# Earlier issue of three x tiles, and a chunk's transposes between the halves of the chunk ahead

## The chip, the cores and the metric

The kernel runs on all 8 cores of one Trainium2 chip, every core with its own data and no communication. The metric is the device time of the slowest core, in microseconds (us). The median before was 841.71 us.

A program on eight cores has a second, slower state: in some executions the cores of one die (cores 0 to 3 or 4 to 7), or of both, get a lower clock for their matrix engine and the time is some per cent longer (about 842 us in fast executions of the kernel before, 868 to 1002 in slow ones; the mean granted clock of a core was 0.98 to 1.00 in fast executions and down to 0.81 in slow ones). Where a profile fell in the slow state, only the cores of the undisturbed die are read.

Names: PE is the TensorE, DVE the VectorE, ACT the ScalarE, POOL the GpSimd engine, SP the engine whose queue issues the tables and most x tiles. SBUF is the memory that the tiles lie in, PSUM the one that matmuls and transposes write. The granted clock is the share of the PE's full clock that the profile records (1.00 is full, 0.50 half).

## The reference, cut to what matters

One layer of a decoder with two gated branches, in float32, with 2048 prompt rows and 64 sample rows per core, so 17 chunks of 128 rows (the last has 64).

```python
h = rms_norm(x, norm_g)
z = h @ w_in                      # nine slices of 1024 columns each
u_a, v_a, gate_a, c_b, b_b, h_b, gate_b, m_a, m_b = split(z)
v_a = layer_norm(gelu(v_a), ln_v_g, ln_v_b)
s   = W_s(group) @ v_a + b_s      # within 128-row chunks
y_a = gelu(u_a) * s * silu(gate_a)
...                               # branch B, merge, output projection, per-layer embedding, final norm
```

The change touches only the first stage of the kernel: normalise x, transpose it (the matmuls of this kernel read h with channels on the partitions), project v, apply GELU and its layer norm. Everything after it starts from the transposed h (`HT`) and the normalised v (`VA`).

## The kernel before

Each engine has one queue of instructions, written out in the order of the Python calls; an instruction waits on semaphores for the buffers that it reads and writes. So the order of calls decides the order on every engine, and that is what the change edits. The helpers of a chunk `c` in the first stage (shortened):

```python
NXI = 6                                   # x tiles in SBUF: tile c lies in slot c % 6
def x_load(c, eng="sp"): ...              # DMA of x rows into XIN[c % 6]
def A0(c): ...  # ACT: square of the tile with row sums; POOL: add eps, power -0.5
def A2(c): ...  # DVE: HTOK = XIN * 1/rms * gain        (1.28 us)
def A3(c): ...  # PE: 8 transposes of HTOK into PSUM
def A4(c): ...  # DVE: copy of the transposes into HT   (0.69 us)
def Bmm(c): ... # PE: 16 matmuls of 512 columns, v of the chunk
def Bact_g(c): ... # ACT: GELU out of PSUM
def Bact_s(c): ... # ACT: square of the GELU with row sums
def C1(c): ...  # DVE: three small operations on the statistics
def C2(c): ...  # POOL: power -0.5
def C3(c): ...  # DVE: one small operation, then VA = normalised v (0.81 us)
```

The opening issues four slices of the v weights and x tiles 2 to 5 on the POOL queue, splits chunk 0 into halves (`A2(0, 0, 1)`, `A2(0, 1, 2)` and so on), and then the sync queue issues four tables before tile 6:

```python
        S._waits("sp", [B_xin[5]], ())    # wait for tile 5
        S.dma("sp", [DMA(cpk[:], cpk_d[:, :])], ...)      # 20 KB
        S.dma("sp", [DMA(bsr[:], ...)], ...)              # 4 KB
        S.dma("sp", [DMA(WST, wsT_d[:, :])], ...)         # 512 KB
        S.dma("sp", [DMA(BC2, ln_b_d.partition_broadcast(128))], ...)   # 512 KB
        ...                                # chunks 0 to 2, slice by slice
        for i in range(4, NCH + 5):
            if 5 <= i - 1 < NCH:
                A2(i - 1)
            if 4 <= i - 2 < NCH:
                A3(i - 2)
                A4(i - 2)
            if 3 <= i - 3 < NCH:
                Bmm(i - 3)
            if okc(i - 5):
                C1(i - 5); C2(i - 5)
            if okc(i - 4):
                Bact_g(i - 4)
            if 5 <= i + 1 < NCH:
                A0(i + 1)
            if okc(i - 4):
                Bact_s(i - 4)
            if okc(i - 5):
                C3(i - 5)
            if NXI <= i + 2 < NCH:
                x_load(i + 2)
            if i == 7: ...    # POOL: select that makes wT from WST
            if i == 8: ...    # DVE: cast of a table to bf16
            if i == 10:
                make_Bd()     # PE: bias table, 16 small matmuls, half of them with one row
            if i == 11: ...   # DVE: copy of the bias table out of PSUM
```

Of the kernel before, what the change touches and what calls it, by code (L numbers as in the profile page):

```python
# [9 lines left out]
ALU = mybir.AluOpType  # L10
# [5 lines left out]
NCH = 17  # L16
# [7 lines left out]
def crow(c):  # L24
    return 128 if c < 16 else 64

def group_chunks(g):
    t0, n = GROUPS[g]
    out = []
    for c in range(NCH):  # L30
        a, b = max(t0, c * 128), min(t0 + n, c * 128 + crow(c))
        if a < b:
            out.append((c, a - c * 128, b - c * 128, a - t0))
    return out
# [119 lines left out]
def STT(out, in0, scalar, in1, op0, op1):  # L154
    return lambda e: e.scalar_tensor_tensor(out=out, in0=in0, scalar=scalar, in1=in1, op0=op0, op1=op1)  # L155
# [6 lines left out]
def CP(out, in_):  # L162
    return lambda e: e.tensor_copy(out=out, in_=in_)
# [7 lines left out]
def build_program(stop_after=99, dbg=()):  # L171
# [31 lines left out]
    with ExitStack() as es:  # L203
# [24 lines left out]
        ps = [es.enter_context(nc.psum_tensor("ps%d" % i, [128, 1024], F32)) for i in range(4)]  # L228
# [7 lines left out]
        S = Sched(nc, es)  # L236
        B_bank = [Buf("bank%d" % i) for i in range(8)]
# [4 lines left out]
        NXI = 6  # L242
        XIN = [MGf[:, i * 1024:(i + 1) * 1024] for i in range(NXI)]
        BC0 = MGf[:, 6144:7168]
        HTOK = [MG[:, 14336:15360], MG[:, 15360:16384], YA[:, 0:1024]]
# [7 lines left out]
        B_xin = [Buf("xin%d" % i) for i in range(NXI)]  # L253
        B_gv = [Buf("gv%d" % i) for i in range(4)]
        B_htok = [Buf("htok0"), Buf("htok1"), Buf("htok2")]
        B_junk = Buf("junk")
        B_bc0h = [Buf("bc0_0"), Buf("bc0_1")]
        B_bc1, B_bc2 = Buf("bc1"), Buf("bc2")
        B_stat = [Buf("stat%d" % c) for c in range(NCH)]
        B_hT = [Buf("hT%d" % c) for c in range(NCH)]  # L260
# [5 lines left out]
        B_ring = [Buf("ring%d" % i) for i in range(NRING)]  # L266
        B_wpp = Buf("wpp")

        def st(c, i, r=128):
            return stat[0:r, c * 16 + i:c * 16 + i + 1]  # L270
# [8 lines left out]
        B_id, B_identb, B_ones, B_blk = Buf("ident"), Buf("identb"), Buf("ones"), Buf("blk")  # L279
# [4 lines left out]
        def x_load(c, eng="sp"):  # L284
            r, t0, sl = crow(c), c * 128, c % NXI
            S.dma(eng, [DMA(XIN[sl][0:r, :], x_d[t0:t0 + r, :])], B_xin[sl] if eng == "sp" else Buf("xsw%d" % c),
                  writes=[B_xin[sl]])
# [6 lines left out]
        def warm(n):  # L294
            S.group("pe", [MM(ps[2][:, 512:1024], JUNK[:, 0:128], JUNK[:, 0:512], True, True) for _ in range(n)], reads=[B_junk])
# [28 lines left out]
        for i, v in ((C_NH, -0.5), (C_DEPS, D * EPS), (C_EPS, EPS)):  # L324
# [4 lines left out]
             writes=[B_id])  # L329
# [7 lines left out]
        for q in range(2):  # L337
            S.op("pe", MM(ps[3][:, q * 512:(q + 1) * 512], ones[0:1, :], GROW[:, q * 512:(q + 1) * 512], True, True),
                 reads=[B_ones, B_gr], writes=[B_bank[6 + q]])
# [10 lines left out]
        HT3 = HT[:, :].rearrange("p (k t) -> p k t", t=NT)  # L350
# [7 lines left out]
            S.op("pool", TT(st(c, 1), st(c, 0), cc(C_EPS), ALU.add), reads=[B_cst], writes=[B_stat[c]])  # L358
            S.op("pool", TT(st(c, 2), st(c, 1), cc(C_NH), ALU.pow), reads=[B_cst], writes=[B_stat[c]])

        def A2(c, q0=0, q1=2):
            r, sl, hs, a, b = crow(c), c % NXI, c % 3, q0 * 512, q1 * 512
            S.op("dve", STT(HTOK[hs][0:r, a:b], XIN[sl][0:r, a:b], st(c, 2, r), BC0[0:r, a:b], ALU.mult, ALU.mult),
                 reads=[B_xin[sl], B_stat[c]] + B_bc0h[q0:q1], writes=[B_htok[hs]])

        def A3(c, q0=0, q1=2):
            r, sl, hs = crow(c), c % 2, c % 3
            pt = bank_bf(sl)
            S.group("pe", [TR(pt[:, k * 128:k * 128 + r], HTOK[hs][0:r, k * 128:(k + 1) * 128], ident[0:r, 0:r])
                           for k in range(4 * q0, 4 * q1)], reads=[B_htok[hs], B_identb], writes=[B_bank[sl]])  # L370

        def A4(c, q0=0, q1=2, own=None):
            r, t0, sl = crow(c), c * 128, c % 2
            pt = bank_bf(sl)
            S.op("dve", CP(HT3[:, 4 * q0:4 * q1, t0:t0 + r],
                           pt.rearrange("p (k t) -> p k t", t=128)[:, 4 * q0:4 * q1, 0:r]),
                 reads=[B_bank[sl]], writes=[own or B_hT[c]])

        B_hT0b = Buf("hT0b")

        def v_pair(c):
            return 1 + c if c < 3 else 1 + (c + 1) % 2
# [1 line left out]
        def Bmm(c, slots=(0, 1, 2, 3)):  # L384
            r, t0, pi = crow(c), c * 128, v_pair(c)
            fns = [MM(ps[pi][0:r, q * 512:(q + 1) * 512], HT[:, k * NT + t0:k * NT + t0 + r],
                      WR[:, k * D + q * 512:k * D + (q + 1) * 512], k == 0, k == 7)
                   for s_ in slots for k in (2 * s_, 2 * s_ + 1) for q in range(2)]
            S.group("pe", fns, reads=[B_hT[c]] + ([B_hT0b] if c == 0 and slots[0] else []) + [B_ring[s_] for s_ in slots],
                    writes=[B_bank[2 * pi], B_bank[2 * pi + 1]] if slots[-1] == 3 else [])  # L390

        def Bact_g(c):
# [57 lines left out]
        x_load(4, "pool")  # L450
        x_load(5, "pool")
        A0(2)
        S._waits("sp", [B_xin[5]], ())
        S.dma("sp", [DMA(cpk[:], cpk_d[:, :])], B_cpk, writes=[B_cpk])
        S.dma("sp", [DMA(bsr[:], b_s_d.rearrange("(o h) t -> o (h t)", o=1))], B_bsr, writes=[B_bsr])
        S.dma("sp", [DMA(WST, wsT_d[:, :])], B_ws, writes=[B_ws])
        S.dma("sp", [DMA(BC2, ln_b_d.partition_broadcast(128))], B_bc2, writes=[B_bc2])

        def bc0(q):
            S.op("dve", CP(BC0[:, q * 512:(q + 1) * 512], ps[3][:, q * 512:(q + 1) * 512]), reads=[B_bank[6 + q]],  # L460
                 writes=[B_bc0h[q]])

        bc0(0)
        A2(0, 0, 1)
        bc0(1)
        A3(0, 0, 1)
        A4(0, 0, 1)
        A2(0, 1, 2)
        Bmm(0, (0,))
        A3(0, 1, 2)  # L470
        A4(0, 1, 2, B_hT0b)
        B_hT[0].inherit(B_hT0b)
        warm(2)
        A2(1)
        A3(1)
        A4(1)
        warm(1)
        Bmm(1, (0,))
        for c in range(2):
            Bmm(c, (1,))  # L480
        A2(2)
        A3(2)
        A4(2)
        for s_ in range(2):
            Bmm(2, (s_,))
        A0(3)
# [10 lines left out]
        for i in range(4, NCH + 5):  # L497
            if 5 <= i - 1 < NCH:
                A2(i - 1)
            if 4 <= i - 2 < NCH:  # L500
                A3(i - 2)
                A4(i - 2)
            if 3 <= i - 3 < NCH:
                Bmm(i - 3)
            if okc(i - 5):
                C1(i - 5)
                C2(i - 5)
# [5 lines that stand above are left out]
                Bact_s(i - 4)  # L513
            if okc(i - 5):
                C3(i - 5)
            if NXI <= i + 2 < NCH:
                x_load(i + 2)
            if i == 7:
                S.op("pool", lambda e: e.affine_select(out=wT3, in_=WST.rearrange("s (h t) -> s h t", t=128),
                                                       pattern=[[0, 8], [1, 128]], compare_op=ALU.is_ge, fill=0.0,  # L520
                                                       base=0, channel_multiplier=-1),
                     reads=[B_ws], writes=[B_wT])
                issue_loads(6)
            if i == 9:
                issue_loads(NRING)
            if i == 8:
                S.op("dve", CP(BC2b, BC2), reads=[B_bc2], writes=[B_bc2b])
            if i == 11:
                S.op("dve", CP(Bd[:, :], ps[3][:, :]), reads=[B_bank[6], B_bank[7]], writes=[B_Bd])
            if i == 10:  # L530
                make_Bd()
                S.dma("sp", [DMA(BC1, ln_g_d.partition_broadcast(128))], B_bc1, writes=[B_bc1])
                S.dma("pool", [DMA(WPP[:, :].rearrange("p (k c) -> p k c", c=D),
                                   w_pp_d.rearrange("(k p) c -> p k c", p=128))], B_wpp, writes=[B_wpp])
            if i == 12:
                emit_blk_dmas()
                S.dma("sp", [DMA(ci_s[:, :], ci0_d[:, :])], B_cis[0], writes=B_cis)

# [9 lines left out]
            return bank(b)[:, 0:GROUPS[g][1]], B_bank[b]  # L548

        def hT_bufs(g):  # L550
            return ([B_hT0b] if g == 0 else []) + [B_hT[c] for (c, _, _, _) in group_chunks(g)]

        def proj(blk_i, c0, g, SRC, src_bufs):
            t0, n = GROUPS[g]
# [19 lines left out]
        if stop_after >= 2:  # L574
# [3 lines left out]
            for h in range(8):  # L578
# [4 lines left out]
                for g in range(5):  # L583
                    t0, n = GROUPS[g]
                    o, ob = proj_hT(bu, hc, g)
                    S.op("act", ACT(T1[:, t0:t0 + n], o, AF.Gelu_apprx_tanh), reads=[ob], writes=[B_t1[g]])
                for g in range(5):
                    t0, n = GROUPS[g]
                    sl = g % 2
# [3 lines left out]
                         reads=[B_t1[g]], writes=[B_t2[sl]])  # L593
                    po, pob = alloc_out(g)
                    fns = []
# [3 lines left out]
                    for (c, la, lb, off) in chs:  # L599
# [4 lines left out]
                        else:  # L604
# [9 lines left out]
                         reads=[pob, B_Bd, B_lngT], writes=[B_tmp[sl]])  # L614
                    if n > npp:
# [3 lines left out]
                             reads=[pob, B_Bd, B_lngT], writes=[B_tmp[sl]])  # L619
                    S.op("dve", TT(YA[:, h * NT + t0:h * NT + t0 + n], tmp[:, 0:n], T2[sl][:, 0:n], ALU.mult),  # L620
                         reads=[B_tmp[sl], B_t2[sl]], writes=[B_ya[h]])
# [6 lines left out]
        if stop_after >= 3:  # L628
# [12 lines left out]
            for j in range(8):  # L641
# [5 lines left out]
                for g in range(5):  # L647
                    t0, n = GROUPS[g]
                    sl = g % 2
# [11 lines left out]
                    else:  # L661
# [5 lines left out]
                         writes=[B_acc[sl]])  # L667
                    S.op("dve", STT(acc[:, 0:npr], ci[:, 1:1 + npr], w1, acc[:, 0:npr], ALU.mult, ALU.add),
                         reads=[B_ci[sl], B_convw], writes=[B_acc[sl]])
                    S.op("dve", STT(acc[:, 0:npr], ci[:, 0:npr], w0, acc[:, 0:npr], ALU.mult, ALU.add),  # L670
                         reads=[B_ci[sl], B_convw], writes=[B_acc[sl]])
                    if g == 4:
                        S.op("pool", CP(cs3[:, j, 0:2], ci[:, npr:npr + 2]), reads=[B_ci[sl]], writes=[B_csall])
                    if has_s:
# [8 lines left out]
                             writes=[B_accs])  # L683
                        S.op("dve", STT(acc3, cj[:, :, 0:4], w0, acc3, ALU.mult, ALU.add), reads=[B_cis[j], B_convw],
                             writes=[B_accs])
# [347 lines left out]
```

## Time and profile before

| | before |
|---|---|
| time, median of the first 3 runs | 841.71 us (841.52 to 842.14) |
| PE busy | 809.4 of 841.0 us (96%) |
| first stage ends | 100.6 us, mean of 8 cores (98.0 to 101.4) |
| longest PE idle time from 38 to 47 us | 3.9 us, mean of 8 cores |

"First stage ends" is, throughout, the start of the first matmul on `ps<-HT,WR`, the next stage's form. The PE never waits long after it (at most 2.04 us at a time before, on core 5, and 1.52 after, on core 7), so a microsecond won in the first stage should be a microsecond of the whole: the mean span less the mean stage end is 837.8 - 100.6 = 737.2 us before, and 834.8 - 98.0 = 736.8 us after.

The timeline of the PE on core 5, the slowest core of this profile, around the first gap. Columns: start in us, duration in us, engine, line (of a helper), operation, output<-inputs, shape, count, and in brackets the idle time before it and what ended it. `L146` are transposes (A3), `ps<-WR,HT` is a chunk's v projection.

```profile
34.85 0.61 PE L146 MATMUL ps<-ident,YA 128*128 128x128 bf16 x8 [0.52 <-DVE YA L155]
35.45 3.61 PE L143 MATMUL ps<-WR,HT 128*128 128x512 bf16 x16
44.45 1.01 PE L146 MATMUL ps<-ident,MG 128*128 128x128 bf16 x8 [5.39 <-DVE MG L155]
45.26 5.50 PE L143 MATMUL ps<-WR,HT 128*128 128x512 bf16 x16
50.60 0.61 PE L146 MATMUL ps<-ident,MG 128*128 128x128 bf16 x8
51.05 3.62 PE L143 MATMUL ps<-WR,HT 128*128 128x512 bf16 x16
...
64.47 6.13 PE L143 MATMUL ps<-WR,HT 128*128 128x512 bf16 x16
70.44 0.61 PE L146 MATMUL ps<-ident,MG 128*128 128x128 bf16 x8
```

The PE stands still for 5.39 us before chunk 6's transposes, and the sixteen matmuls after that take 5.50 us instead of 3.62. The matmuls at 64.47 follow the bias table and are slow too (6.13 us).

The row of the windows view for the same core (window, its length, busy time of PE, weight loads, DVE, ACT, POOL, then granted clock, DMA share, GB/s) shows the clock:

```profile
35.00:45.00 10.00, 4.61 (x30) 2.36 (x29) 3.58 (x10) 6.90 (x13) 2.90 (x5) 0.86 0.96 295
45.00:58.00 13.00, 12.91 (x66) 5.99 (x64) 9.74 (x20) 10.90 (x22) 7.47 (x14) 0.84 1.00 213
```

Why chunk 6 is late is in two more timelines of the same core, first that of the sync queue:

```profile
27.16 0.33 SPq L169 DMA_DIRECT2D cpks<-cpk  x1
27.53 0.42 SPq L169 DMA_DIRECT2D bsr<-b_s  x1
28.00 0.36 SPq L169 DMA_DIRECT2D YA<-wsT  x1
28.40 0.42 SPq L169 DMA_DIRECT2D YA<-ln_b  x1
29.04 15.57 SPq L169 DMA_DIRECT2D MG<-x  x7
```

Then that of ACT, with the square of tile 6:

```profile
38.10 1.06 ACT L149 ACTIVATE MG<-MG 128x1024 bf16<-128x1024 f32 x1 [6.83 <-DMA MG<-x]
```

Tile 5 lands at 27.1, four tables go first, tile 6 is issued at 29.04, and ACT waits 6.83 us for it. The square of tile 6 then starts the chain of statistics, multiply, transposes.

A second thing shows in the same profile, late in the stage: DVE's copies of the transposes (A4).

```profile
75.48 0.68 DVE L163 COPY HT<-ps 128x1024 bf16<-128x1024 bf16 x1
...
77.60 0.16 DVE L155 SCALAR_TENSOR_TENSOR stat<-stat 128x1 f32<-128x1 f32 x1 [0.80 <-POOL stat L152]
...
79.79 0.68 DVE L163 COPY HT<-ps 128x1024 bf16<-128x1024 bf16 x1
```

They follow each other at 4.31 us, with no wait for another engine except 0.80 us in each round for POOL's power (C2). The PE needs 3.9 us for a chunk. Before, nothing was lost by that: between a chunk's transposes and its matmuls stood the sixteen matmuls of the chunk ahead (3.5 us from start to start), so DVE could fall that far behind. Its copy starts 0.72 us after the transposes at 70.44 and 3.0 us after those at 89.94, and soon after that the stage ends.

### The profile page before, as it was taken

Reading aid. Unit: us, or ns where it says so; the run is one execution under the profiler, and the core shown is the slowest. Engines: PE = TensorE matmul, PEld = TensorE weight load, DVE = VectorE, ACT = ScalarE, POOL = GpSimd, SP = SyncE. Lnnn points to the kernel's source line nnn. Section 1 sums busy time; section 2 is a strip of 40 time slices with the busy share of each in tenths; the row PEclk is TensorE's granted clock in tenths of the full one; section 3 lists DMA queues with packets and bytes.
Section 4 is the critical chain, followed back from the end, with each engine's and each line's share of the span. In section 5 each row is a group of like instructions: output and inputs, shape, how many; then the busy total and the mean of one; then the engine's idle time right before and its main releaser. Section 6 shows DMA issues by size and latency. Waiting matters only on the chain.

```text
span 841.0 us, 14209 instructions; the slowest of 8 cores (834.3 to 841.0 us)
## 1 busy us (share of the span) xinstructions
PE 809.4 (96%) x4563; PEld 431.9 (51%) x4563; DVE 445.4 (53%) x728; ACT 301.1 (36%) x517; POOL 117.5 (14%) x257
## 2 busy tenths in 40 slices
PE   5789999999999999999999999999999999999994
PEld 2345455555554555455555545554555454444441
DVE  4376675646665555555555323332333246777774
ACT  2476645554432333232332111111111124545552
POOL 4153210000000100101001001000010012323331
PEclk8988999999999999999999999999999999999998
DMA  9895073302300410600603406005032762344311
GB/s 185 219 219 113 1 140 49 51 13 40 51 1 1 76 26 1 101 1 5 97 1 55 79 1 101 1 12 90 1 57 45 97 191 90 135 148 139 122 76 62
DMA packets 21338, 60.78 MB, mean 72 GB/s; under 512 B 2770, under 2 KB 7058, under 8 KB 21268
## 3 DMA queue, kind: packets, MB, share of 16 engines
q0 software_dynamic: 10352, 29.89, 22.8%
q1 hardware_dynamic: 10914, 29.99, 11.4%
q8 instruction: 40, 0.66, 0.3%
q14 instruction: 30, 0.25, 0.1%
q10 hardware_dynamic: 2, 0.00, 0.0%
HBM read 78.08 MB, written 9.58 MB: 104 GB/s over the span
## 4 chain that ended last, share of the span: by engine, by line
PE 92%; DMA 3%; DVE 1%; ACT 1%; issue 1%; POOL 1%; POOLq 0%; DVEq 0%; SPq 0%; ACTq 0%
PE ps L143 90%; DMA MG<-x 2%; PE ps L146 2%; DMA YA<-pe_g 1%; DVE YA L155 1%; ACT SCR L149 1%; ACT YA L149 0%; POOL stat L152 0%; ACT MG L149 0%; POOL WR L169 0%; DVE MG L155 0%; DVE WR L155 0%; DVE YA L152 0%; DVE VA L155 0%; DVE YA L159 0%
## 5 line engine op out<-in xcount | busy, mean ns | idle before, releaser
L143 PE MATMUL ps<-HT,WR 128*128 128x512 bf16 (+2 forms) x2560 | 469.7, 342 | 0.0
L143 PEld LDWEIGHTS ps<-HT,WR 128*128 128x128 bf16 x2560 | 248.4, 98 | 200.7 <-issue 0.4
L149 ACT ACTIVATE SCR<-ps 128x512 f32<-128x512 f32 (+2 forms) x240 | 123.9, 520 | 324.0 <-PE ps L143 268.4
L155 DVE SCALAR_TENSOR_TENSOR SCR<-SCR,ps 128x512 f32<-128x512 f32 (+2 forms) x80 | 47.5, 594 | 151.2 <-PE ps L143 151.2
L152 POOL TENSOR_TENSOR stat<-stat,cst 128x1 f32<-128x1 f32 x119 | 68.3, 576 | 178.4 <-ACT SCR L149 105.2
L152 DVE TENSOR_TENSOR SCR<-SCR,ps 128x512 f32<-128x512 f32 (+2 forms) x88 | 48.1, 547 | 46.5 <-PE ps L143 38.1
L155 DVE SCALAR_TENSOR_TENSOR SCR<-SCR,cpks 128x512 f32<-128x512 f32 (+1 forms) x80 | 51.5, 644 | 38.0 <-ACT SCR L149 27.8
L143 PE MATMUL ps<-WR,HT 128*128 128x512 bf16 (+1 forms) x272 | 66.8, 402 | 4.2 <-DMA WR<-w_v 2.4
L143 PE MATMUL ps<-HT 128*128 128x512 bf16 (+1 forms) x272 | 61.6, 379 | 2.3 <-ACT HT L149 2.3
L143 PE MATMUL ps<-YA,WR 128*128 128x512 bf16 (+2 forms) x320 | 63.6, 342 | 0.0
L143 PE MATMUL ps<-VA,WR 128*128 128x512 bf16 (+2 forms) x320 | 63.6, 342 | 0.0
L143 PE MATMUL ps<-WR,MG 128*128 128x512 bf16 (+1 forms) x272 | 62.5, 384 | 0.0
L169 POOL DMA_DIRECT2D WR<-wt x44 | 24.0, 546 | 274.3 <-PE ps L143 272.5
L149 ACT ACTIVATE SCR<-SCR,cpks 128x512 f32<-128x512 f32 (+1 forms) x40 | 25.5, 637 | 60.5 <-DVE SCR L152 60.5
L143 PEld LDWEIGHTS ps<-WR,HT 128*128 128x128 bf16 (+1 forms) x272 | 27.2, 103 | 36.9 <-issue 11.8
L152 DVE TENSOR_TENSOR SCR<-SCR 128x512 f32<-128x512 f32 (+2 forms) x40 | 23.7, 592 | 41.5 <-ACT SCR L149 41.5
L143 PEld LDWEIGHTS ps<-VA,WR 128*128 128x128 bf16 x320 | 31.3, 98 | 25.8
L143 PEld LDWEIGHTS ps<-YA,WR 128*128 128x128 bf16 x320 | 31.3, 98 | 25.8
L143 PEld LDWEIGHTS ps<-WR,MG 128*128 128x128 bf16 (+1 forms) x272 | 27.0, 100 | 32.6 <-issue 2.0
L143 PEld LDWEIGHTS ps<-HT 128*128 128x128 bf16 (+1 forms) x272 | 25.9, 98 | 31.0 <-issue 3.3
L155 DVE SCALAR_TENSOR_TENSOR YA<-YA,ps 128x1024 f32<-128x1024 f32 (+1 forms) x17 | 20.7, 1220 | 21.2 <-ACT YA L149 21.2
L152 DVE TENSOR_TENSOR VA<-SCR 128x512 bf16<-128x512 f32 (+2 forms) x48 | 25.2, 526 | 7.7 <-DVE SCR L152 5.0
(85 smaller groups left out, 549.4 us busy)
## 6 DMA issues: line engine op xcount, KB each, us to landing
WR<-wt POOLq DMA_DIRECT2D x44, 512.0 KB, 9.0
y<-YA SPq DMA_DIRECT2D x16, 512.0 KB, 2.9
MG<-x SPq DMA_DIRECT2D x12, 512.0 KB, 9.7
WR<-x SPq DMA_DIRECT2D x8, 512.0 KB, 4.4
VA<-x SPq DMA_DIRECT2D x8, 512.0 KB, 4.3
WR<-w_v POOLq DMA_DIRECT2D x4, 512.0 KB, 12.2
MG<-x POOLq DMA_DIRECT2D x4, 512.0 KB, 14.5
SCR<-p SPq DMA_DIRECT2D x16, 128.0 KB, 4.2
```

Source lines behind the costliest of these rows:

```text
L143: return lambda e: e.matmul(out, lhsT=lhsT, rhs=rhs, start=start, stop=stop)
L146: return lambda e: e.transpose(out, in_, idn)
L149: return lambda e: e.activation(out=out, in_=in_, func=func, **kw)
L152: return lambda e: e.tensor_tensor(out=out, in0=in0, in1=in1, op=op)
L155: return lambda e: e.scalar_tensor_tensor(out=out, in0=in0, scalar=scalar, in1=in1, op0=op0, op1=op1)
L169: return lambda e: e.dma_start(out=out, in_=in_)
```

## The change

Its intent: let the DMA engines fetch tiles 6 to 8 in the pause that the tables' turn left (41 GB/s from 27 to 30 us on core 5, against 295 from 35 to 45), and hide the wait for a chunk's transposes behind the second half of the chunk ahead. The opening works in whole tiles instead of halves, and the table work moves two rounds later. The core of the diff, shortened:

```diff
-        S._waits("sp", [B_xin[5]], ())
+        S._waits("sp", [B_xin[4]], ())
+        for c in range(6, 9):
+            x_load(c)
         S.dma("sp", [DMA(cpk[:], cpk_d[:, :])], B_cpk, writes=[B_cpk])
 ...
-        bc0(0)
-        A2(0, 0, 1)
-        bc0(1)
-        A3(0, 0, 1)
-        A4(0, 0, 1)
-        A2(0, 1, 2)
-        Bmm(0, (0,))
-        ...
+        warm(9)
+        A2(0)
+        A2(1)
+        A3(0)
+        A4(0)
+        A3(1)
+        A4(1)
+        for s_ in range(2):
+            for c in range(2):
+                Bmm(c, (s_,))
 ...
             if 5 <= i - 1 < NCH:
                 A2(i - 1)
+            if 3 <= i - 3 < NCH:
+                Bmm(i - 3, (0, 1))
             if 4 <= i - 2 < NCH:
                 A3(i - 2)
                 A4(i - 2)
             if 3 <= i - 3 < NCH:
-                Bmm(i - 3)
+                Bmm(i - 3, (2, 3))
 ...
-            if NXI <= i + 2 < NCH:
-                x_load(i + 2)
+            if NXI + 3 <= i + 5 < NCH:
+                x_load(i + 5)
 ...          # select i == 7 -> 9, cast 8 -> 10, make_Bd 10 -> 12, its copy 11 -> 13, and so on
```

`Bmm` also got a wait for its PSUM banks at the start of the first half.

More of the change, by code (lines that the diff above doesn't have):

```diff
@@ L359, in A0, with A2, A3 @@
             S.op("pool", TT(st(c, 2), st(c, 1), cc(C_NH), ALU.pow), reads=[B_cst], writes=[B_stat[c]])
-        def A2(c, q0=0, q1=2):
-            r, sl, hs, a, b = crow(c), c % NXI, c % 3, q0 * 512, q1 * 512
-            S.op("dve", STT(HTOK[hs][0:r, a:b], XIN[sl][0:r, a:b], st(c, 2, r), BC0[0:r, a:b], ALU.mult, ALU.mult),
-                 reads=[B_xin[sl], B_stat[c]] + B_bc0h[q0:q1], writes=[B_htok[hs]])
-        def A3(c, q0=0, q1=2):
+        def A2(c):
+            r, sl, hs = crow(c), c % NXI, c % 3
+            S.op("dve", STT(HTOK[hs][0:r, :], XIN[sl][0:r, :], st(c, 2, r), BC0[0:r, :], ALU.mult, ALU.mult),
+                 reads=[B_xin[sl], B_stat[c]] + B_bc0h, writes=[B_htok[hs]])
+        def A3(c):
             r, sl, hs = crow(c), c % 2, c % 3
@@ L369, in A3, with A4 @@
             S.group("pe", [TR(pt[:, k * 128:k * 128 + r], HTOK[hs][0:r, k * 128:(k + 1) * 128], ident[0:r, 0:r])
-                           for k in range(4 * q0, 4 * q1)], reads=[B_htok[hs], B_identb], writes=[B_bank[sl]])
-        def A4(c, q0=0, q1=2, own=None):
+                           for k in range(8)], reads=[B_htok[hs], B_identb], writes=[B_bank[sl]])
+        def A4(c):
             r, t0, sl = crow(c), c * 128, c % 2
             pt = bank_bf(sl)
-            S.op("dve", CP(HT3[:, 4 * q0:4 * q1, t0:t0 + r],
-                           pt.rearrange("p (k t) -> p k t", t=128)[:, 4 * q0:4 * q1, 0:r]),
-                 reads=[B_bank[sl]], writes=[own or B_hT[c]])
-        B_hT0b = Buf("hT0b")
+            S.op("dve", CP(HT3[:, :, t0:t0 + r], pt.rearrange("p (k t) -> p k t", t=128)[:, :, 0:r]),
+                 reads=[B_bank[sl]], writes=[B_hT[c]])
         def v_pair(c):
@@ L388, in Bmm @@
                    for s_ in slots for k in (2 * s_, 2 * s_ + 1) for q in range(2)]
-            S.group("pe", fns, reads=[B_hT[c]] + ([B_hT0b] if c == 0 and slots[0] else []) + [B_ring[s_] for s_ in slots],
+            if slots[0] == 0:
+                S._waits("pe", (), [B_bank[2 * pi], B_bank[2 * pi + 1]])
+            S.group("pe", fns, reads=[B_hT[c]] + [B_ring[s_] for s_ in slots],
                     writes=[B_bank[2 * pi], B_bank[2 * pi + 1]] if slots[-1] == 3 else [])
@@ L452, in build_program @@
         A0(2)
-        S._waits("sp", [B_xin[5]], ())
+        for q in range(2):
+            S.op("dve", CP(BC0[:, q * 512:(q + 1) * 512], ps[3][:, q * 512:(q + 1) * 512]), reads=[B_bank[6 + q]],
+                 writes=[B_bc0h[q]])
+        warm(9)
[8 more added lines that the diff above has]
+                Bmm(c, (s_,))
+        A2(2)
+        A3(2)
+        A4(2)
+        S._waits("sp", [B_xin[4]], ())
+        for c in range(6, 9):
+            x_load(c)
         S.dma("sp", [DMA(cpk[:], cpk_d[:, :])], B_cpk, writes=[B_cpk])
@@ L457, in build_program @@
         S.dma("sp", [DMA(BC2, ln_b_d.partition_broadcast(128))], B_bc2, writes=[B_bc2])
-        def bc0(q):
-            S.op("dve", CP(BC0[:, q * 512:(q + 1) * 512], ps[3][:, q * 512:(q + 1) * 512]), reads=[B_bank[6 + q]],
-                 writes=[B_bc0h[q]])
-        bc0(0)
-        A2(0, 0, 1)
-        bc0(1)
-        A3(0, 0, 1)
-        A4(0, 0, 1)
-        A2(0, 1, 2)
-        Bmm(0, (0,))
-        A3(0, 1, 2)
-        A4(0, 1, 2, B_hT0b)
-        B_hT[0].inherit(B_hT0b)
-        warm(2)
-        A2(1)
-        A3(1)
-        A4(1)
-        warm(1)
-        Bmm(1, (0,))
-        for c in range(2):
-            Bmm(c, (1,))
-        A2(2)
-        A3(2)
-        A4(2)
         for s_ in range(2):
@@ L515, in build_program @@
                 C3(i - 5)
-            if NXI <= i + 2 < NCH:
-                x_load(i + 2)
-            if i == 7:
+            if NXI + 3 <= i + 5 < NCH:
+                x_load(i + 5)
+            if i == 9:
                 S.op("pool", lambda e: e.affine_select(out=wT3, in_=WST.rearrange("s (h t) -> s h t", t=128),
@@ L523, in build_program @@
                 issue_loads(6)
-            if i == 9:
+            if i == 11:
                 issue_loads(NRING)
-            if i == 8:
+            if i == 10:
                 S.op("dve", CP(BC2b, BC2), reads=[B_bc2], writes=[B_bc2b])
-            if i == 11:
+            if i == 13:
                 S.op("dve", CP(Bd[:, :], ps[3][:, :]), reads=[B_bank[6], B_bank[7]], writes=[B_Bd])
-            if i == 10:
+            if i == 12:
                 make_Bd()
@@ L534, in build_program @@
                                    w_pp_d.rearrange("(k p) c -> p k c", p=128))], B_wpp, writes=[B_wpp])
-            if i == 12:
+            if i == 14:
                 emit_blk_dmas()
@@ L550, in hT_bufs @@
         def hT_bufs(g):
-            return ([B_hT0b] if g == 0 else []) + [B_hT[c] for (c, _, _, _) in group_chunks(g)]
+            return [B_hT[c] for (c, _, _, _) in group_chunks(g)]
         def proj(blk_i, c0, g, SRC, src_bufs):
```

## The prediction

> **What bounds it now.** The busy table gives the TensorE 809.4 of 841.0 us (96%); the chain of waits puts 92% of the span on it. What can be won is in the first stage (normalise, transpose, project v), which by the timeline ends at 101.4 us on the slowest core (98.0 to 101.4 by core); the other 737 to 740 us are not touched. A chunk costs the TensorE 3.9 us there, so what follows the start of chunk 4 at 35.45 needs 13 x 3.9 + 5.0 (bias table) = 55.7 us and takes 66. The excess: 5.4 us idle before chunk 6's transposes (2.0 to 5.4 by core), because x tile 6 lands at 38.05; 1.9 us of half-speed matmuls after that gap (16 in 5.50 instead of 3.62); 2.5 us of half speed after the bias table. [...] granted clock 0.50 from 45 to 48 us.
>
> Tile 6 is late because the sync queue waits for tile 5 (27.1 us), then issues four tables first; DMA moves 41 GB/s from 27 to 30 us.
>
> **What the change does.**
> 1. Tiles 6 to 8 are issued when tile 4 has landed (25.85). Estimate from landings here: tile 6 lands at 30 to 32. The long gap goes.
> 2. The opening works in whole tiles: chunk 0 starts 0.5 to 1 us later, but the last two slices of the v weights land at 21 and 24 us in both kernels. The opening block ends 1 to 3 us earlier, at 27 to 29.
> 3. That is not kept in full. Tile 4's landing starts a chain that both kernels have: square, GELU of chunk 0, square of tile 5, square of the GELU, statistics, normalise, VectorE's multiply of chunk 5 (33.3), and queued behind it the copy of chunk 4's transposes (34.5). Chunk 4 starts near 35 as before on the slowest core, 2 us earlier where it started at 37.
> 4. From there VectorE sets the pace. Its copies follow each other at 4.31 us (75.48, 79.79, 84.31, 88.62), above the TensorE's 3.9. Before, a copy had a chunk's matmuls (3.5 us) of slack; with the transposes inside a chunk it has half. So I expect idle gaps of 0.4 us before each of chunks 5 to 9.
> 5. The bias table moves from after chunk 7 to after chunk 9; its 5.0 and 2.5 us stay.
>
> Sum for the slowest core: copy of chunk 4 at 34.5; six periods of 4.31, plus 0.85 (the multiply that took 2.12 instead of 1.28 us beside GpSimd's select) and 0.6 (table cast) give 61.8 for chunk 10's copy; the table ends at 67.4, then seven chunks of 3.9 plus 2.5: 97.5, or 3.9 us less than 101.4. If idle time before chunk 4 trips the half clock, 1.3 us of it is lost.
>
> **Predicted: 838.2 us, range 835.5 to 841.5.** Faster by over 2%: 0.01; within 2%: 0.985; slower by over 2%: 0.005.
>
> **What would show it.** Step 1: no TensorE idle over 3 us in 38 to 46 us. Step 3: chunk 4's copy still at 34 to 35. Step 4: copies 4.3 us apart from 35 to 58, TensorE waiting for each. Step 5: 16 matmuls in about 6 us after the table. First stage ending at 96 to 99.
>
> **What would make it wrong.** Tiles 5 to 8 contending so that tile 5 is late (slower); copies not setting the pace, so that chunks take 3.9 us (2 to 3 us faster); idle time in the opening keeping the clock at half speed; a different granted clock over the later 740 us.

What was measured: granted clock 0.50 from 45 to 48 us on core 5 of the kernel before. The sum came to 97.5 us for the end of the stage. The 1.3 us for a half clock before chunk 4 stands outside the sum, as the author's estimate. Core 6 of the kernel before shows a loss of that size: after its gap of 3.75 us, chunk 6's sixteen matmuls took 4.87 us instead of 3.62.

## The result, and the profile after

The changed kernel took 838.78 us (838.28 to 839.11, 4 runs) against 841.83 us of the kernel before in the same rounds. The ratio is 0.9963, 95% interval 0.9946 to 0.9981. Ratios are the mean time of one kernel's fast runs over that of the other's fast runs of the same rounds, so not quite the ratio of the quoted medians. A second set of rounds later (after_again) gave 0.9970 (0.9957 to 0.9983). The forecast was 838.2 us. What was written before the second set:

> The changed kernel once more, so that it shares a chip and rounds with the runs below. Ratio to before 0.996 again (0.9946 to 0.9981 on record).

| means of 8 cores in the profile, us | before | after |
|---|---|---|
| first stage ends | 100.6 | 98.0 |
| bias table starts / ends on the PE | 58.6 / 63.7 (after chunk 7) | 61.9 / 67.1 (after chunk 9) |
| from the table's end to the stage's end | 37.0 (9 chunks) | 31.0 (7 chunks) |
| longest PE idle time from 38 to 47 us | 3.9 | 0.2 |
| PE waits over 0.15 us from the table to the stage's end, in total | 0.0 | 1.4 |

The timeline of the PE on core 5 after the change. Matmuls of a chunk now come as two eights with the next chunk's transposes between them:

```profile
30.69 1.89 PE L143 MATMUL ps<-WR,HT 128*128 128x512 bf16 x8
35.02 1.89 PE L143 MATMUL ps<-WR,HT 128*128 128x512 bf16 x8 [2.44 <-DVE stat L159]
36.74 0.61 PE L146 MATMUL ps<-ident,YA 128*128 128x128 bf16 x8
37.19 1.89 PE L143 MATMUL ps<-WR,HT 128*128 128x512 bf16 x8
39.33 1.89 PE L143 MATMUL ps<-WR,HT 128*128 128x512 bf16 x8 [0.26 <-DVE stat L159]
...
53.12 1.89 PE L143 MATMUL ps<-WR,HT 128*128 128x512 bf16 x8 [1.10 <-DVE stat L159]
...
66.55 3.02 PE L143 MATMUL ps<-WR,HT 128*128 128x512 bf16 x8
...
76.84 1.89 PE L143 MATMUL ps<-WR,HT 128*128 128x512 bf16 x8 [0.65 <-DVE stat L159]
...
81.15 1.89 PE L143 MATMUL ps<-WR,HT 128*128 128x512 bf16 x8 [0.26 <-DVE stat L159]
```

The gap of 5.39 us is gone. In its place stand 2.44 us before chunk 4 and a small wait before every chunk. The releaser reads `stat L159`, a tiny DVE operation that starts just before the copy is shown to end (34.79 against 34.87 us before chunk 4); what the PE waits for is DVE's count at the copy `HT<-ps` just before it. A run below with another order in that queue names the copy itself.

The windows rows of the same core that answer to those of before:

```profile
35.00:45.00 10.00, 9.47 (x55) 4.54 (x56) 6.83 (x17) 7.90 (x15) 3.95 (x8) 1.00 0.90 301
45.00:58.00 13.00, 10.83 (x67) 5.14 (x65) 10.61 (x20) 9.92 (x21) 6.21 (x10) 1.00 0.58 124
```

Its sync queue:

```profile
26.15 1.38 SPq L169 DMA_DIRECT2D MG<-x  x3
27.58 1.01 SPq L169 DMA_DIRECT2D cpks<-cpk  x1
```

And ACT's timeline, with the square of tile 6:

```profile
31.58 1.06 ACT L149 ACTIVATE MG<-MG 128x1024 bf16<-128x1024 f32 x1 [0.23 <-DMA MG<-x]
```

Tile 6 is issued 2.9 us earlier and used 6.5 us earlier, and ACT waits 0.23 us for it. PE busy time from 35 to 45 us doubles, and falls again from 45 to 58, where the small waits are.

DVE's queue on core 5 after the change, multiplies (`L155`) and copies (`L163`); the rows between them, statistics and normalisation of an older chunk, are left out:

```profile
32.26 0.81 DVE L160 TENSOR_SCALAR VA<-YA,stat 128x1024 bf16<-128x1024 f32 x1
32.99 1.28 DVE L155 SCALAR_TENSOR_TENSOR YA<-MG,stat 128x1024 bf16<-128x1024 f32 x1
34.19 0.68 DVE L163 COPY HT<-ps 128x1024 bf16<-128x1024 bf16 x1
...
38.50 0.68 DVE L163 COPY HT<-ps 128x1024 bf16<-128x1024 bf16 x1
...
42.82 0.68 DVE L163 COPY HT<-ps 128x1024 bf16<-128x1024 bf16 x1
...
50.26 2.12 DVE L155 SCALAR_TENSOR_TENSOR MG<-MG,stat 128x1024 bf16<-128x1024 f32 x1
52.30 0.68 DVE L163 COPY HT<-ps 128x1024 bf16<-128x1024 bf16 x1
```

From 34.19 the copies stand 4.31 us apart, and each of the PE's small waits ends just after one of them. The one multiply of 2.12 us runs beside POOL's select (49.97 to 51.30).

### The profile page after: what moved, and what is told of

Its sections match the earlier page's. It is cut to its first block, busy times and chain, and to the rows that moved or that the text cites. A ratio compares the mean times of both kernels' runs of the same rounds, so it can differ in the third digit from the quotient of the medians.

```text
span 836.9 us, 14194 instructions; the slowest of 8 cores (832.9 to 836.9 us)
## 1 busy us (share of the span) xinstructions
PE 810.0 (97%) x4569; PEld 431.7 (52%) x4569; DVE 445.8 (53%) x726; ACT 301.0 (36%) x517; POOL 116.6 (14%) x257
## 4 chain that ended last, share of the span: by engine, by line
PE 88%; DMA 3%; issue 3%; DVE 3%; ACT 1%; POOL 1%; DVEq 0%; POOLq 0%; SPq 0%; ACTq 0%
PE ps L143 86%; DMA MG<-x 2%; PE ps L146 1%; DMA YA<-pe_g 1%; POOL stat L152 1%; DVE HT L163 1%; DVE YA L155 1%; ACT YA L149 0%; ACT SCR L149 0%; DVE stat L155 0%; DVE MG L155 0%; DVE stat L160 0%; ACT MG L149 0%; POOL WR L169 0%; DVE YA L152 0%
## 5 line engine op out<-in xcount | busy, mean ns | idle before, releaser
L155 DVE SCALAR_TENSOR_TENSOR SCR<-SCR,ps 128x512 f32<-128x512 f32 (+2 forms) x80 | 47.6, 594 | 151.1 <-PE ps L143 151.1
L143 PE MATMUL ps<-WR,HT 128*128 128x512 bf16 (+1 forms) x272 | 68.8, 404 | 6.6 <-DVE stat L159 5.5
L155 DVE SCALAR_TENSOR_TENSOR SCR<-SCR,cpks 128x512 f32<-128x512 f32 (+1 forms) x80 | 51.6, 645 | 37.6 <-ACT SCR L149 27.8
L155 DVE SCALAR_TENSOR_TENSOR YA<-YA,ps 128x1024 f32<-128x1024 f32 (+1 forms) x17 | 20.7, 1220 | 21.7 <-ACT YA L149 21.7
```

The costliest lines, as they stand in the source:

```text
L143: return lambda e: e.matmul(out, lhsT=lhsT, rhs=rhs, start=start, stop=stop)
L155: return lambda e: e.scalar_tensor_tensor(out=out, in0=in0, scalar=scalar, in1=in1, op0=op0, op1=op1)
```

## The experiments

Theory: the order of the loads carries the whole gain. With tile 6 there in time, DVE's serial queue sets the pace (4.31 us a chunk), because it waits inside every round for POOL. Rival: the interleaved transposes carry about half of the gain, by hiding a wait of the PE; or the pace after the gap is the PE's or the loads' own. Every run below gave correct results. "Stage end" is the mean over the cores of the profiled run.

| run | edit | stage end | ratio to before (95% interval) |
|---|---|---|---|
| before | | 100.6 | 1 |
| after | the whole change | 98.0 | 0.9963 (0.9946 to 0.9981) |
| after_again | the same, later rounds | 98.2 | 0.9970 (0.9957 to 0.9983) |
| loads_only | before + loads | 96.5 | 0.9945 (0.9930 to 0.9960) |
| interleave_only | before + interleaving | 104.0 | 1.0043 (1.0027 to 1.0058) |
| after_old_loads | after - loads | 103.9 | 1.0037 (1.0022 to 1.0052) |
| after_not_interleaved | after - interleaving | 95.8 | 0.9930 (0.9913 to 0.9947) |
| after_copy_first | after, DVE order | 96.5 (die 1) | one fast run |
| after_c3_late (and _2) | after, DVE round shortened | 91.8 (die 1) | 0.9904 (0.9887 to 0.9922) |
| after_both (and _2) | after, both DVE edits | 92.9 | 0.9903 (0.9878 to 0.9927) |
| noint_both | not interleaved, both DVE edits | 92.9 | 0.9901 (0.9886 to 0.9917) |
| noint_both_spread | the same, bias table spread out | 89.4 | 0.9861 (0.9847 to 0.9875) |

The share of slow executions was not the same in all kernels. Most runs of after_c3_late, after_copy_first, after_both and noint_both were slow (7 of 8, 7 of 8, 8 of 9 and 4 of 7 in their first rounds; 5 of 7 and 4 of 6 when after_c3_late and after_both were repeated), against 4 of 22 for the kernel before in the same rounds and 0 of 4 for noint_both_spread. Why is left open. Their ratios above rest on few fast runs (two each for the repeated sets, three for noint_both). The runs were made in three sets of rounds on different chips, each beside the kernel before, and a ratio compares within its own set. The stage end of after_both is that of the fast profile of its second set.

### Parts of the change, alone and left out

**loads_only**: the kernel before with the loads' order alone.

```diff
-        S._waits("sp", [B_xin[5]], ())       # with the tables, before chunk 0
+        S._waits("sp", [B_xin[4]], ())       # after chunk 2's copy in program order
+        for c in range(6, 9):
+            x_load(c)
         ...tables...
-            if NXI <= i + 2 < NCH:
-                x_load(i + 2)
+            if NXI + 3 <= i + 5 < NCH:
+                x_load(i + 5)
```

> The kernel before with only tiles 6 to 8 issued ahead of the tables (opening in halves and transposes at the head of a chunk kept). Theory (load order carries the gain, VectorE sets the pace after it): the idle time before chunk 6's transposes falls from 2.0 to 5.4 us to under 1 us; copies of transposes about 4.3 us apart from chunk 4 on; first stage ends at 96.5 to 99 us; time 2.5 to 3.5 us below before, so 838.3 to 839.3. Rival (the interleaved transposes carry about half of the gain): the time is only about 1.5 us below before.

Measured: 837.05 us median, ratio 0.9945, a gain of 4.6 us on 842 us. This one part gains more than the whole change did in either set of rounds. The stage ends at 96.5 us, the low edge of what was expected. The longest idle time between 38 and 47 us is 0.84 us, on core 5 before chunk 7's transposes:

```profile
40.98 0.61 PE L146 MATMUL ps<-ident,MG 128*128 128x128 bf16 x8
41.69 3.61 PE L143 MATMUL ps<-WR,HT 128*128 128x512 bf16 x16
46.14 0.61 PE L146 MATMUL ps<-ident,MG 128*128 128x128 bf16 x8 [0.84 <-DVE MG L155]
```

Chunk 6's transposes, at 40.98, have no wait left. The edit moves two things at once: tiles 6 to 8 go ahead of the tables, and they wait for tile 4 instead of tile 5. No run separates them.

**interleave_only**: the kernel before with the transposes moved.

```diff
+            if 3 <= i - 3 < NCH:
+                Bmm(i - 3, (0, 1))
             if 4 <= i - 2 < NCH:
                 A3(i - 2)
                 A4(i - 2)
             if 3 <= i - 3 < NCH:
-                Bmm(i - 3)
+                Bmm(i - 3, (2, 3))
```

> The kernel before with only the transposes moved between the halves of the chunk ahead. Theory: the gap that waits for tile 6 stays (over 2 us on most cores), nothing is gained, and up to 1 us is lost after the bias table because VectorE's copy has half the slack; first stage ends at 101 to 103 us, time 841.5 to 843.5. Rival: the interleaving alone gives about half of the gain, 840.3.

Measured: 845.26 us, ratio 1.0043, stage end 104.0. The rival falls: the interleaving gains nothing alone, it loses 3.6 us, more than the theory's 1 us. The gap for tile 6 stays as expected. Two losses stand in the profile: the PE waits 2.1 us in total after the table (mean of 8 cores, 0.0 before), and a wait of 2.1 to 2.7 us before chunk 4 is followed by half clock on all eight cores; no core of the kernel before shows half clock between 30 and 42 us.

**after_not_interleaved**: the changed kernel with the lines above undone.

> The changed kernel with the transposes back at the head of the chunk. Theory: same pace of 4.31 us up to the bias table, then chunks at 3.9 us instead of 4.31, because VectorE is let go right after the table; first stage ends 0.6 to 1.0 us earlier than in the changed kernel (96.3 to 96.8 instead of 97.3 on a core like its core 5); time 837.5 to 838.3. Rival: the idle time of TensorE before each chunk grows and the time rises by about 1.5 us to 840.3.

Measured: 835.75 us, ratio 0.9930. The changed kernel had 0.9963 and 0.9970, so the interleaving costs it 0.0033 to 0.0040, or 2.8 to 3.4 us (2.2 us in the stage ends of the two profiles). These ratios come from different sets of rounds; the intervals just touch with the first and are apart with the second. The direction was the theory's, the size about three times what it expected. The means over the cores show where it is lost: the bias table starts at the same time in both (61.7 and 61.9 us), and from its end to the stage's end it is 29.1 us here and 31.0 in the changed kernel. The PE of this run on core 7 after the table:

```profile
66.68 0.67 PE L146 MATMUL ps<-ident,YA 128*128 128x128 bf16 x8
67.14 5.29 PE L143 MATMUL ps<-WR,HT 128*128 128x512 bf16 x16
72.27 0.61 PE L146 MATMUL ps<-ident,MG 128*128 128x128 bf16 x8
72.72 3.62 PE L143 MATMUL ps<-WR,HT 128*128 128x512 bf16 x16
```

The transposes of the next chunk come first after the table, so DVE can copy them while the PE works slowly on the sixteen matmuls; from then on DVE has a lead and no bracket with idle time appears. In the changed kernel the first eight slow matmuls (3.02 us at 66.55 above) come before the transposes, DVE stands idle for 4.57 us until it can copy, and then the PE waits for it in each chunk (0.65, then 0.26 us). DVE on core 5 of the changed kernel:

```profile
70.53 0.69 DVE L163 COPY HT<-ps 128x1024 bf16<-128x1024 bf16 x1 [4.57 <-PE ps L146]
```

**after_old_loads**: the changed kernel with the sync queue's order of before.

> The changed kernel with the loads of x tiles as before (tables first, waiting for tile 5). Theory: the gap before chunk 6 comes back, ACT waits for tile 6 until about 38 us, and nearly the whole gain goes, whatever the opening and the transposes do: first stage ends at 100.5 to 102.5 us, time 841 to 843. Rival: half of the gain stays, 840.3.

Measured: 844.69 us, ratio 1.0037, stage end 103.9, slower than expected (841 to 843) by 1.7 us and more. Without the loads' order the rest of the change is a loss, as in interleave_only (1.0043). No help from the new opening shows there: the two intervals overlap almost wholly.

What the opening is worth with the early loads in place is the difference between loads_only and after_not_interleaved: 0.9945 against 0.9930, and stage ends of 96.5 against 95.8. That is 0.7 us in the profiles and about 1.3 us in the times, but the intervals overlap, so it is not shown.

### DVE's queue

**after_c3_late**: the normalisation of a finished v chunk one round later, so that POOL's power is long done when DVE comes to it.

```diff
-            if okc(i - 5):
-                C3(i - 5)
+            if okc(i - 6):
+                C3(i - 6)
-        for i in range(4, NCH + 5):
+        for i in range(4, NCH + 6):
```

> The changed kernel with VectorE's normalisation of a finished v chunk one iteration later, so that VectorE no longer waits 0.8 us for GpSimd's power inside each chunk; nothing else moved. Theory (VectorE's serial queue sets the pace from chunk 4 on): the spacing of the copies falls from 4.31 to TensorE's 3.9 us, the 0.26 us idle gaps before chunks go, chunk 4 starts 1 to 2 us earlier because its copy is no longer queued behind the normalisation of chunk 0; first stage ends at 91 to 94 us (changed kernel 96.7 to 99.3), ratio to before 0.989 to 0.991. Rival (the pace is TensorE's or the loads'): copies still 4.3 us apart or the stage end within 1 us of the changed kernel, ratio 0.996.

> The run with the normalisation one iteration later again, because all but one of its timed runs fell in the slow state. Its profile already showed copies 3.5 to 4.0 us apart and first stages ending at 90.1 to 93.0 us on the undisturbed cores. Theory: ratio 0.989 to 0.991. Rival (pace not VectorE's): 0.996.

Measured: two fast runs in the second set give 0.9904; one in the first took 832.68 us. Die 1 of the first profile was undisturbed; its stages end at 91.8 us on average. DVE's copies on its core 7:

```profile
36.89 0.68 DVE L163 COPY HT<-ps 128x1024 bf16<-128x1024 bf16 x1
40.42 0.69 DVE L163 COPY HT<-ps 128x1024 bf16<-128x1024 bf16 x1
44.32 0.69 DVE L163 COPY HT<-ps 128x1024 bf16<-128x1024 bf16 x1 [0.34 <-PE ps L146]
```

They are 3.5 and 3.9 us apart, and now DVE waits for the PE's transposes (0.34 us) instead of the other way round. No operation was removed; one was put off by a round. That shows that DVE's round set the pace of the changed kernel. The shift also moved POOL's select clear of DVE's multiplies, which saves the 0.84 us of the long multiply once. Chunk 4 starts at 33.48 instead of 35.0 us on this core.

**after_copy_first**: the copy of a chunk's transposes ahead of the next chunk's multiply on DVE.

```diff
-            if 5 <= i - 1 < NCH:
-                A2(i - 1)
             if 3 <= i - 3 < NCH:
                 Bmm(i - 3, (0, 1))
             if 4 <= i - 2 < NCH:
                 A3(i - 2)
                 A4(i - 2)
+            if 5 <= i - 1 < NCH:
+                A2(i - 1)
```

> The changed kernel with VectorE's copy of a chunk's transposes queued ahead of the multiply of the next chunk. Theory: the wait before chunk 4 shrinks by about 1.2 us (the multiply's length), the pace stays 4.3 us, so the first stage ends about 1 us earlier and the ratio to before is about 0.995. If the order inside VectorE's queue were what costs the interleaved version its time, the stage would end 2 to 3 us earlier, ratio 0.993.

Measured: only one fast run, 836.38 us, with no interval. On the undisturbed die the wait before chunk 4 is 1.25 us instead of 2.44, the copies on its core 7 stay 4.32 us apart, and the stage ends at 96.5 us, 1.1 us earlier than on the same die of the changed kernel (97.6). The PE's waits now name the copy:

```profile
38.27 1.89 PE L143 MATMUL ps<-WR,HT 128*128 128x512 bf16 x8 [0.26 <-DVE HT L163]
```

So the order cost about what was expected at chunk 4, and the pace is untouched by it. How much of the time it gives is not settled by one run.

**after_both** and **noint_both**: both DVE edits, with and without the interleaving.

> Both VectorE edits on the changed kernel. Theory: chunk 4 starts near 32.5 us, chunks then follow at 3.9 us; first stage ends at 90 to 92.5 us, ratio to before 0.987 to 0.990. Rival (pace not VectorE's): ratio 0.995 to 0.996.

> Both VectorE edits with interleaved transposes again, for fast runs. Theory: ratio within 0.001 of the version without interleaving (0.9901), so 0.988 to 0.991. Rival (interleaving costs time by itself on TensorE): 0.993.

> Both VectorE edits on the changed kernel without the interleaved transposes. Theory: with VectorE faster than TensorE the place of the transposes costs or gains nothing any more, so within 0.7 us of the run with both edits and interleaved transposes. Rival (the interleaving costs 2 to 3 us by itself, on TensorE): 2 to 3 us faster than that run.

Measured: 0.9903 with (two fast runs of the second set), 0.9901 without (three fast runs). Stage ends 92.9 in both. The rival, that the interleaving costs PE time by itself, would have put them 2 to 3 us apart; it falls. The interleaving costs time only while DVE is slower than the PE. The expected extra of after_both over after_c3_late did not come: 0.9903 against 0.9904, with two fast runs each. In the profile of after_both_2 the PE waits up to 3.4 us (core 6) for DVE between 38 and 47 us, and at most 0.9 on the undisturbed cores of after_c3_late; so on some cores the copy's new place costs again what it won at chunk 4.

### What is left in the stage: the bias table

**noint_both_spread**: the table's eight heads made one per chunk.

```diff
-            if i == 12:
-                make_Bd()                 # all eight heads, 16 matmuls in a row
+            if 12 <= i <= 19:
+                make_Bd(i - 12)           # one head after Bmm(i - 3)
-            if i == 13: ...               # copy of the table out of PSUM
+            if i == 20: ...
```

> Loads first, transposes at the head of the chunk, both VectorE edits, and the bias table's eight heads made one per chunk instead of all at once. Theory: what runs at half clock after the table (about 2 us) is due to 4.6 to 5 us of single-row matmuls in one stretch, so spread out it goes: 16 matmuls of a chunk stay at 3.6 us, the first stage ends at 90 to 92 us, 2 us earlier than without the spreading (91.6 to 93.9), ratio to before 0.987 to 0.989. Rival (half clock comes from elsewhere, or the spread pieces wait for something): stage end unchanged or later, ratio 0.990 or more.

Measured: 829.53 us (829.32 to 830.27, all 4 runs fast), ratio 0.9861, stage end 89.4 us. It is the fastest version, 11.7 us below the 841.24 us of the kernel before in its rounds. The gain over noint_both is 3.6 us at the stage's end (89.39 against 92.95), more than the 2 us expected; 0.6 of it is there before the first head (57.9 against 58.5 us), the rest comes after. The sixteen matmuls after the table in noint_both, on its core 7:

```profile
65.28 5.20 PE L143 MATMUL ps<-WR,HT 128*128 128x512 bf16 x16
```

The PE of core 0 of noint_both_spread, where one head follows chunk 9:

```profile
59.15 0.22 PE L143 MATMUL ps<-wT,YA 128*128 128x128 bf16 x1
59.30 0.48 PE L143 MATMUL ps<-bsr,ones 1*128 1x128 f32 x2
59.72 0.62 PE L146 MATMUL ps<-ident,YA 128*128 128x128 bf16 x8
60.17 3.62 PE L143 MATMUL ps<-WR,HT 128*128 128x512 bf16 x16
63.63 0.22 PE L143 MATMUL ps<-wT,YA 128*128 128x128 bf16 x1
```

The sixteen matmuls stay at 3.62 us. That single rows are the cause of the half clock, as the expectation has it, is not shown (last section). A head costs 59.72 - 59.15 = 0.57 us, so the eight cost 4.6 us, about as much as the table in one piece (61.95 to 66.55 on core 5 of the changed kernel); what goes is the slow stretch after it (5.20 against 3.62 us). The edit also puts off DVE's copy of the table; after the first head the PE waits for DVE in neither run, so that is not where the gain comes from.

## Why the prediction was right, point by point

- **The time.** 838.2 us forecast, 838.78 measured. The stage was to end at 97.5 us on a core like core 5, and core 5 ended at 97.34. That close agreement is partly luck: the slowest core went from 101.4 to 99.3 us, the mean from 100.6 to 98.0, so 2.1 and 2.6 us against the 3.9 forecast. The stretch of half clock around the table's end lasted 3.4 us on cores 0, 4, 5 and 6 (stage end 97.0 on average) and 6.8 us on the other four (99.0).
- **Step 1, the gap.** Right. No PE idle time over 0.3 us between 38 and 46 us on core 5; tile 6 used at 31.58, in the range of 30 to 32 given for its landing. loads_only and after_old_loads show that this is the part that carries the gain.
- **Step 2, the opening.** The block ended at 27.9 us on core 5, within 27 to 29. But chunk 0's first matmul came at 13.96 instead of 11.52 us, 2.4 us later and not "0.5 to 1". The warm-up matmuls alone took 4.02 us on this core. It did not matter on this core, because the PE then waits for the last slice of the weights all the same (0.33 us, until 24.67).
- **Step 3, the chain from tile 4.** Right: the copy of chunk 4 at 34.19 (forecast 34.5), the chunk at 35.02. The wait of 2.44 us (2.36 on core 7) was followed by half clock on cores 0, 6 and 7 (the next eight matmuls took 2.55 to 3.24 us instead of 1.89), and not on the other five; what separates them is not shown (last section). That was named as a risk.
- **Step 4, DVE's pace.** Right in mechanism: 4.31 us between copies, and 10 waits for DVE in the stage on core 5; chunk 10's copy was forecast for 61.8 us and came at 61.54. The waits show as 0.26 us rather than 0.4 in an ordinary round, though the round itself is longer by the 0.41 us forecast (4.31 less 3.9): eight matmuls before a wait are shown for 1.89 us, but follow-on work starts after 1.72, as at 35.02 and 36.74. after_c3_late shows the cause by taking it away.
- **Step 5, the mis-sized term.** The last term of the sum, "then seven chunks of 3.9 plus 2.5", is 29.8 us after the table and took 30.8 on core 5 (31.0 on average). What the term left out is 1.42 us of waits for DVE after the table on core 5 (1.4 on average), which the prediction expected only before it. Part of that was made good: the half clock cost about 1.7 us on core 5 instead of 2.5 (66.55 to 73.85 is 7.30 us for work of 5.63 at full clock), and chunk 10's transposes (0.45) already stood before the table. Two other slips hid the rest: the table ended at 66.55, not 67.4, and 67.4 plus 29.8 is 97.2, which the text gave as 97.5.
- **What it did not say.** It treated the change as one gain with a part not kept. The runs show a gain of 4.6 us from the loads (loads_only) and a loss of about 3 us from the interleaving (after_not_interleaved against after). The prediction saw that the transposes inside a chunk halve the copy's slack, but placed the cost wrongly: it charged it to chunks 5 to 9. after_not_interleaved reaches the table at the same time (61.7 against 61.9 us), so that loss is DVE's pace wherever the transposes stand; what the interleaving itself costs comes after the table (1.9 us), where the prediction charged nothing.

Two observations carry the reasoning. DVE works through its queue in order: on core 5 of the changed kernel chunk 4's transposes are done at 30.85 us, but their copy starts at 34.19, behind a multiply (32.99, 1.28 us) that has nothing to do with it, and after_copy_first shortens the PE's wait for it from 2.44 to 1.25 us by order alone. And a multiply of DVE beside POOL's select takes longer: 2.12 instead of 1.28 us for the multiply of x and gain, on all 8 cores of both kernels. On all 8 cores of after_c3_late, where the select meets no such multiply, none is longer than 1.3 us.

## What to carry to other kernels

When a change with several parts moves the time a little, run each part alone: here one part gained 4.6 us and another gave about 3 of them back. Before moving work inside the busiest engine's queue to hide a wait, measure the round of the engine that feeds it; if that engine's round (4.31 us) is longer than the busiest engine's own (3.9), shorten the round first, for instance by putting off an operation that waits for a third engine. After every long stretch on the busiest engine, queue first what sets the other engines going again.

## What the traces show of the clock, and of DVE beside POOL

- The length of a gap does not by itself decide whether half clock follows. In the changed kernel all eight cores stood still for 2.36 to 2.44 us before chunk 4. On cores 0, 6 and 7 the granted clock was then 0.50 for 3.41 us (eight matmuls in 2.55 to 3.24 us instead of 1.89); on the other five it stayed at 1.00, though the shortest gap, of 2.36 us, was core 7's. 2.1 us in interleave_only was followed by half clock (cores 1, 2, 3, 4 and 7), 3.41 us on core 6 of after_both_2 was not. What separates these cases is not shown.
- The PE is shown busy without a break through the bias table, half of whose matmuls have one row, and yet the granted clock is 0.65 from 66 to 70 us on core 5 of the changed kernel. With the table spread between full matmuls, the sixteen matmuls of each chunk between the heads stay at 3.62 to 3.64 us (noint_both_spread, core 0, 55.70 to 90.03 us). Whether the single row, the float32 or the small size is at fault, no run separates.
- In the fast runs, with the PE busy for 96% of the span on the slowest core, the mean granted clock is 0.98 to 1.00 on all eight cores, and sixteen matmuls take 3.46 us from start to start (60.17 to 63.63 above). The lowest mean clock is 0.81 for one core in the 1002 us execution of the kernel before.
- The multiply of 1.28 us took 0.84 us more when it lay beside the select for 1.04 us; the select took 1.33 us instead of the 1.09 of after_c3_late. In after_copy_first an overlap of 0.44 us made the multiply 0.24 longer (1.52 us).
